# Chunk products of an RWKV-7 recurrence: from tiles of the array to the full array, with both heads moving

## The chip, the cores and the metric

The kernel runs on one core of a Trainium2 chip. The metric is the device time of one execution in microseconds (us). The engines are TensorE (PE in the profile; its weight loads are shown apart as PEld), VectorE (DVE), ScalarE (ACT), GpSimd (POOL) and SyncE (SP), which issues the DMAs. Each takes its own instructions in the order in which they were written.

## The reference

Two layers over 528 tokens (16 learned tokens and 512 of the input) of width 1024. Layer 0 is an RWKV-7 mixer with 32 heads of 64, layer 1 is latent attention with 16 heads. What the change touches is the recurrence of layer 0; for every head it is

```
def step(S, inp):
    r_t, w_t, k_t, v_t, a_t, b_t = inp
    sa = einsum('bhij,bhj->bhi', S, a_t)
    S = S * w_t[:, :, None, :] + sa[..., None] * b_t[:, :, None, :] + v_t[..., None] * k_t[:, :, None, :]
    return S, einsum('bhij,bhj->bhi', S, r_t)
```

ahead of it stand the projections of the tokens to v, k, r and a gate g (each 16 tiles of 128 columns), behind it a normalisation, the gate and an output projection.

## The kernel before

**Recurrence in chunks.** The 528 steps are cut into nine chunks, one of 16 steps (chunk 0) and eight of 64. The 32 heads go in 16 pairs; head 0 of a pair lies on partitions 0 to 63 (`H0`), head 1 on 64 to 127 (`H1`). For each pair p the work goes through these stages, each a Python generator that yields small steps:

- `prepare` makes from k, r, the decays and the rates the operands `KB` and `ALR` of all chunks;
- `within` calls `products(p)`: per chunk and head a product of `KB` and `ALR`, masked on DVE into `Qf` (the triangular matrix M to be inverted), `MR` and a part of `ALR`;
- `sides` makes `SV` (state and values) and `KBt`;
- `invert(0)` and `invert(1)` are two lanes that invert M in fp16 by doubling, chunks 0 to 3 and 4 to 8; the last product of a lane writes the inverse over `Qf` (event `within`);
- `ends(0)`, `recur` and `ends(8)` call `chunk` for chunk 0, for chunks 1 to 7 and for chunk 8. A chunk has the products `ALR` by `SV` (into `xs`), `SV` by `ALR` (output), `Qf` by `xs` (into `SV`), `KBt` by `SV` (the next state), `SV` by `MR` (output). The first, third and fourth depend on one another. Chunk 8's output addition sets the event `recur`, and `finish` normalises.

Every chunk product is fp32 and is made of two matmuls, one for each head, on a part of the array: 128 rows by 64 columns, or 64 by 64. One such matmul is two records in the trace. The inverses are fp16 on 128 by 128, the projections fp32r on 128 by 128 with 264 moving columns, three matmuls in a row for each piece (`pg<-x,w`).

**Buffers.** `tl(n, shape, tag)` takes the next of n buffers. `Qf` and `MR` have three, so `products(p)` waits for the event `recur` of pair p-3 (`within`).

**Order.** `Flow` records the instructions and picks, step by step, the one with the earliest start by its own table of costs (`cost`, `LAGS`); between equals the stage that stands first in the list wins (finish, recur, ends, sides, invert, within, prepare, ..., projections last). `hungry` brings a wide matmul forward by `AHEAD`. The order is then fixed in the program. The projections of k and r for pair p can't run far ahead, since `out_k` waits for the event `prepare` of pair p-2. The 16 gate projections come after the last r.

Of the kernel before, what the change touches and what calls it, by code (L numbers as in the profile page):

```python
# [60 lines left out]
class K:  # L61
# [14 lines left out]
    def consts(self):  # L76
        nc = self.nc
        cp = self.cp = self.pool("consts", 1)
        self.par = cp.tile([128, Par.n], F32, name="par")
        self.ones, self.ident, self.center = (cp.tile([128, 128], F32, name=n) for n in ("ones", "ident", "center"))  # L80
        self.bones = cp.tile([128, 128], F32R, name="bones")
        self.omka = cp.tile([128, NP], F32, name="omka")
        nc.gpsimd.memset(self.ones, 1.0)
        for name, x in (("eps_gn", GN_EPS), ("one", 1.0), ("eps_rms", RMS_EPS)):
            t = cp.tile([128, 1], F32, name=name)
            setattr(self, name, t)
            nc.gpsimd.memset(t, x)
# [41 lines left out]
class Flow:  # L129
# [9 lines left out]
    SLACK = 0.0  # L139
# [80 lines left out]
    def cost(eng, method, out, ins, point):  # L220
# [3 lines left out]
        if eng == "tensor":  # L224
# [7 lines left out]
            if w.dtype == F32:  # L232
                if m == 64 and out.base_partition():
                    return [(0.02, m / 1.2e3, 2 * n * r)]
                return [(n / 1.2e3, m / 1.2e3, (2 if m > 64 else 1) * n * r)] * 2
# [99 lines left out]
    def run(self, stages):  # L335
        stages = [[g, None, None] for g in stages]
        while True:
            best, known = None, len(self.events)
            for i, s in enumerate(stages):
# [20 lines left out]
                for j in range(len(s[1])):  # L360
# [3 lines left out]
                    if s[1][j].wide and self.hungry(t):  # L364
                        t -= self.AHEAD
# [33 lines left out]
class Layer0:  # L399
# [57 lines left out]
    def norm(self):  # L457
# [3 lines left out]
        for bufs, tag, n in ((2, "SV", 2), (2, "KBt", 2), (3, "MR", 2), (1, "KB", 2), (3, "ALR", 3), (3, "ALR", 3)):  # L461
            t = tl(bufs, (128, 576 * n), tag)
            wide += [t[:, 576 * i : 576 * i + 576] for i in range(n)]
        wide += [tl(2, (128, 529), "vx") for _ in range(2)]
# [11 lines left out]
        part = [tl(1, (128, T), "P"), tl(2, (128, T), "gx")]  # L476
# [33 lines left out]
    def place(self):  # L510
# [3 lines left out]
        for bufs, tag, n in ((2, "SV", 2), (2, "KBt", 2), (3, "MR", 2), (3, "MR", 2), (3, "ALR", 3)):  # L514
            t = tl(bufs, (128, 576 * n), tag, R)
            wide += [t[:, 576 * i : 576 * i + T] for i in range(n)]
        qf = [tl(3, (128, T), "Qf", R) for _ in range(3)]
        self.lora = {4: qf[0], 5: tl(1, (128, T), "bvl", R)}
        self.spare = wide.pop(10)
        self.places = wide + qf[1:] + [tl(2, (128, T), "Y", R) for _ in range(2)]  # L520
# [45 lines left out]
    def units(self):  # L566
# [5 lines left out]
        self.feed.third([u[0] for u in self.feed.units[0][:AHEAD]], lambda: self.tl(1, (128, 512), "yl"))  # L572
# [47 lines left out]
    def out_v(self, j, out):  # L620
        o = self.tl(2, (128, T), "gx")
# [93 lines left out]
    def out_g(self, p, out):  # L715
# [8 lines left out]
        if p >= 8:  # L724
            if p >= 10:
                yield self.flow.until(("gate", p - 2))
            s = tl(2, (128, T), "gx")
# [60 lines left out]
    def prepare(self):  # L788
        g, nc, tl = self.g, self.nc, self.tl
        yield self.flow.until(("lerps", 0), ("lerps", 1), "decays2")  # L790
        for p in range(NP):
# [53 lines left out]
            ALR = s["ALR"] = tl(3, (128, 9, 3, 64), "ALR")  # L845
            nc.gpsimd.memset(KB[:, 0, :, NM:64], 0.0)
            nc.gpsimd.memset(ALR[:, 0, :, NM:64], 0.0)
            yield
            for x, y, s0 in ((tmp, IP, 1), (kk, at, 0)):
# [6 lines left out]
            for hs, z, eng in ((H0, 0, nc.vector), (H1, 2, nc.gpsimd)):  # L856
# [4 lines left out]
            nc.vector.tensor_tensor(ALR[:, 1:9, 1, :], xm, P[:, 1:9, 1:65], ALU.mult)  # L861
            nc.gpsimd.tensor_tensor(ALR[:, 0, 1, 0:NM], x0, P[:, 0, 1 : NM + 1], ALU.mult)
            yield
# [11 lines left out]
    def within(self):  # L875
        for p in range(NP):
# [3 lines left out]
            if p >= 3:  # L880
                yield self.flow.until(("recur", p - 3))
# [53 lines left out]
    def products(self, p):  # L935
# [4 lines left out]
        MR = s["MR"] = tl(3, (128, 9, 2, 64), "MR")  # L940
        M = s["Qf"] = tl(3, (128, 9, 64), "Qf")
        self.flow.cut[M.tensor.name] = CUT * 64
        nc.gpsimd.memset(MR[:, 0, :, NM:64], 0.0)
        nc.gpsimd.memset(M[:, 0, NM:64], 0.0)
        flat = lambda t: t.rearrange("p s t -> p (s t)")
        for c0 in (1, 5):
# [3 lines left out]
            for j in range(4):  # L950
                for i, hs in enumerate((H0, H1)):
                    nc.tensor.matmul(qv[i][:, j, :, :], flat(KB[hs, c0 + j]), ALR[hs, c0 + j, i : i + 2, :], start=True, stop=True)
# [8 lines left out]
        for i, hs in enumerate((H0, H1)):  # L961
            q = self.one()
            gm.append((q, q[:, 0 : 2 * NM].rearrange("p (s t) -> p s t", t=NM)))
            nc.tensor.matmul(gm[i][1], flat(KB[hs, 0]), ALR[hs, 0, i : i + 2, 0:NM], start=True, stop=True)
        yield
        for i, (q, v) in enumerate(gm):
            for dst, src, m in self.masked(i, M[:, :, 0:NM], MR[:, :, :, 0:NM], ALR[:, :, :, 0:NM], 0, v.unsqueeze(1)):
# [3 lines left out]

    def masked(self, i, M, MR, ALR, cs, qv):

        hs, other, z = ((H0, H1, 0), (H1, H0, 2))[i]
        return ((M[hs, cs, :], qv[hs, :, i, :], self.mS[hs]), (MR[:, cs, i, :], qv[:, :, 1 - i, :], self.mI),
                (ALR[other, cs, z, :], qv[other, :, i, :], self.mS[other]))
# [46 lines left out]
    def inverse(self, p, lane):  # L1023
# [6 lines left out]
        nc.scalar.activation(Mh, M, AF.Copy)  # L1030
        yield
        for hs in (H0, H1):
            nc.gpsimd.tensor_tensor(Lb[hs, :, hs], M[hs], Mh[hs], ALU.subtract)
# [65 lines left out]
        nc.vector.scalar_tensor_tensor(M, v, -1.0, Q, ALU.mult, ALU.subtract)  # L1099
# [4 lines left out]
    def chunk(self, p, ci, small, xs, y, taken):  # L1104
# [3 lines left out]
        ALR, SV, KBt, MR, Qf = (s[x] for x in ("ALR", "SV", "KBt", "MR", "Qf"))  # L1108
        PC = s["PC"][:, ci : ci + 1]
        n = NM if ci == 0 else 64  # L1110
        heads = ((H0, 0), (H1, 1))
        q = small()
        x = q[:, 0:64]
        nc.tensor.matmul(x[H0], ALR[:, ci, 0, :], SV[:, ci, 0, :], start=True, stop=True)
        nc.tensor.matmul(x[H1], ALR[:, ci, 2, :], SV[:, ci, 1, :], start=True, stop=True)
        nc.vector.tensor_copy(xs, x)
        if ci < 8:
            nc.last(x)
        if ci:
            v = y() if ci < 8 else q[:, 64:128]  # L1120
            for hs, h in heads:
                nc.tensor.matmul(v[hs], SV[hs, ci, h, :], ALR[hs, ci, 1, 0:n], start=True, stop=(ci == 8))
            if ci == 8:
                nc.scalar.activation(s["Y"][:, T - 64 :], v, AF.Copy)
# [7 lines left out]
        for hs in (H0, H1):  # L1132
            nc.tensor.matmul(x[hs], Qf[hs, ci, :], xs[hs], start=True, stop=True)
# [4 lines left out]
        if ci < 8:  # L1138
            x = small()[:, 0:64]
            nc.tensor.matmul(x[H0], KBt[:, ci, 0:64], SV[:, ci, 0, :], start=True, stop=True)  # L1140
            nc.tensor.matmul(x[H1], KBt[:, ci, 64:128], SV[:, ci, 1, :], start=True, stop=True)
            for hs, h in heads:
                if ci:
                    nc.vector.scalar_tensor_tensor(SV[hs, ci + 1, h, :], x[hs], PC[hs], sd[hs], ALU.mult, ALU.add)
                else:
                    nc.vector.tensor_scalar(SV[hs, ci + 1, h, :], x[hs], PC[hs], None, ALU.mult)
# [3 lines left out]
        for hs, h in heads:  # L1150
            nc.tensor.matmul(v[hs], SV[:, ci, h, :], MR[:, ci, h, 0:n], start=(ci in (0, 8)), stop=True)
# [4 lines left out]
    def recur(self):  # L1156

        nc, tl = self.nc, self.tl
        for p in range(NP):
# [3 lines left out]
            for cs in ((1, 2, 3, 4), (5, 6, 7)):  # L1163
                yp = self.psum("py", 512, 1)
                for i, ci in enumerate(cs):
# [3 lines left out]
                    def taken(y):  # L1169
                        if ci == cs[-1]:  # L1170
                            n = 64 * len(cs)
                            t0 = NM + 64 * (cs[0] - 1)
                            nc.scalar.activation(Y[:, t0 : t0 + n], yp[:, 0:n], AF.Copy)
                            nc.last(yp)

                    yield from self.chunk(p, ci, small, tl(2, (128, 64), "xs"), lambda: yp[:, 64 * i : 64 * i + 64], taken)

    def ends(self, ci):

        nc, tl, flow = self.nc, self.tl, self.flow  # L1180
        for p in range(NP):
# [9 lines left out]
            def taken(y):  # L1191
                if ci == 0:
                    nc.scalar.activation(Y[:, 0:NM], y, AF.Copy)
                else:
                    nc.vector.tensor_tensor(Y[:, T - 64 :], Y[:, T - 64 :], y, ALU.add)
# [3 lines left out]
            yield from self.chunk(p, ci, self.one, tl(2, (128, 64), "xs"), lambda: self.one()[:, 0 : 64 if ci else NM], taken)  # L1199

    def finish(self):
        g, nc, tl = self.g, self.nc, self.tl
        for p in range(NP):
# [7 lines left out]
            for q, v, ts in (yield from self.headsum(sq, "bvl", "yl", nc.gpsimd)):  # L1211
# [952 lines left out]
```

## Time and profile before

| | us |
|---|---|
| median of three runs | 1615.7 (1611.27 to 1623.01) |
| the profiled execution, its own time | 1630.59 |
| its span, first to last instruction | 1628.6 |
| PE busy in the span | 1498.6 (92%) |
| DVE, ACT, POOL busy | 1006.9, 967.1, 806.3 |

Up to about 206 us the kernel projects v and prepares, from there to 993 us it runs the recurrence with the projections of k, r and g between, and after that the output projection and layer 1. Busy time of PE is modelled from pipelined records, so the distance from one start to the next tells more than a record's own duration. All instructions carry the line of the recording helper (L293), so that groups are told apart by the names of their tiles, as out<-moving,stationary.

### The profile page before, as it was taken

The numbers are of one execution on the slowest core, as the hardware profiler recorded it, in microseconds if no ns is written. First come the engines' busy times: TensorE is split into PE (matmuls) and PEld (weight loads), VectorE is DVE, ScalarE is ACT, GpSimd is POOL, SyncE is SP. The second block draws the span as 40 slices with busy tenths as digits, with TensorE's granted clock in tenths as the row PEclk, the third lists the DMA queues.
The fourth block names the chain that finished last, engine by engine and source line by source line (L and its number), as shares of the span: only waits on it lengthen the run. The fifth ranks groups of instructions, "written<-read, shape, count | busy, mean of one in ns | idle before, by whom it ended". The sixth has DMA issues, their size and how long they took to land. (4 is left out here: it accounts for less than half of the span.)

```text
span 1628.6 us, 36087 instructions
## 1 busy us (share of the span) xinstructions
PE 1498.6 (92%) x13788; PEld 1292.3 (79%) x13788; DVE 1006.9 (62%) x2144; ACT 967.1 (59%) x2451; POOL 806.3 (50%) x1039
## 2 busy tenths in 40 slices
PE   4889889999999999998899999999989999999997
PEld 3889878777877877777787889998778888877786
DVE  7994677788778678777664542035366666666503
ACT  3557657876767677775686865445454544544532
POOL 5353566566556465554565565745522222332554
PEclk8999999999989899998897999999989999999999
DMA  3446522122112121121402247532211111111332
GB/s 112 143 173 230 188 85 87 41 68 74 68 58 71 42 77 65 61 81 55 167 35 73 86 139 256 159 110 92 68 52 40 56 46 52 59 56 43 110 93 82
DMA packets 84700, 148.66 MB, mean 91 GB/s; under 512 B 9392, under 2 KB 18480, under 8 KB 84528
## 3 DMA queue, kind: packets, MB, share of 16 engines
q1 hardware_dynamic: 84528, 146.37, 27.7%
q8 instruction: 108, 1.77, 0.4%
q14 instruction: 64, 0.52, 0.1%
HBM read 112.87 MB, written 33.46 MB: 90 GB/s over the span
## 5 line engine op out<-in xcount | busy, mean ns | idle before, releaser
L293 POOL TENSOR_TENSOR w<-wraw,w 128x512 fp32r<-128x512 f32 (+1 forms) x278 | 358.7, 1296 | 431.3 <-ACT w L293 393.5
L293 PE MATMUL pg<-x,w 128*128 128x264 f32 x2256 | 401.7, 310 | 5.3 <-ACT k L293 3.9
L293 PEld LDWEIGHTS pg<-x,w 128*128 128x128 f32 x2256 | 313.1, 196 | 21.1 <-ACT k L293 4.9
L293 ACT ACTIVATE w<-wraw 128x512 fp32r<-128x512 f32 (+1 forms) x278 | 169.6, 616 | 154.1 <-DMA wraw<-wo 51.0
L293 POOL TENSOR_TENSOR sd<-SV,PC 64x64 f32<-64x64 f32 x224 | 80.7, 360 | 73.8 <-DVE SV L293 63.9
L293 PE MATMUL pb<-u,w 128*128 128x512 f32 x384 | 106.4, 410 | 5.3 <-DVE sg L293 5.3
L293 PE MATMUL pg<-lat,w 128*128 128x512 f32 (+1 forms) x480 | 109.4, 370 | 0.0
L293 DVE SCALAR_TENSOR_TENSOR SV<-pc,PC,sd 64x64 f32<-64x64 f32 x224 | 63.2, 282 | 55.3 <-PE pc L293 49.0
L293 PEld LDWEIGHTS pg<-lat,w 128*128 128x128 f32 x480 | 82.2, 201 | 10.6
L293 PEld LDWEIGHTS pb<-u,w 128*128 128x128 f32 x384 | 71.4, 196 | 19.6 <-DVE sg L293 6.0
L293 PE MATMUL pg<-O,w 128*128 128x512 f32 x336 | 81.7, 401 | 1.8 <-DVE O L293 1.2
L293 ACT ACTIVATE SV<-pc 64x64 f32<-64x64 f32 x224 | 48.4, 216 | 49.5 <-PE pc L293 41.0
L293 PEld LDWEIGHTS pg<-O,w 128*128 128x128 f32 x336 | 63.8, 192 | 17.1 <-DVE O L293 2.0
L293 PEld LDWEIGHTS <-Mb 128*128 128x128 f16 x1152 | 51.9, 98 | 20.8 <-issue 4.5
L293 DVE TENSOR_TENSOR Xs<-pw,masks 128x128 f16<-128x128 f32 (+1 forms) x160 | 48.0, 305 | 30.5 <-PE pw L293 18.6
L293 POOL TENSOR_TENSOR Lb<-Qf,Mh 64x256 f16<-64x256 f32 (+1 forms) x64 | 50.7, 793 | 28.4 <-ACT Mh L293 23.9
L293 DVE SCALAR_TENSOR_TENSOR sg<-sg,par,rs 128x264 f32<-128x264 f32 x32 | 15.6, 518 | 73.5 <-ACT rs L293 73.5
L293 ACT ACTIVATE Qb<-pw 128x256 f16<-128x256 f32 (+1 forms) x128 | 51.8, 410 | 15.3 <-PE pw L293 13.7
L293 PE MATMUL pw<-Tm,Mb 128*128 128x32 f16 (+1 forms) x864 | 55.8, 183 | 4.9 <-DVE Tm L293 4.2
L293 ACT ACTIVATE PT<-py 128x128 fp32r<-128x128 f32 (+1 forms) x64 | 27.9, 436 | 53.6 <-PE py L293 53.6
L293 ACT ACTIVATE Tm<-pw 128x128 f16<-128x128 f32 (+1 forms) x160 | 44.9, 288 | 24.2 <-PE pw L293 22.0
L293 DVE TENSOR_TENSOR sg<-sg,rs 128x256 f32<-128x256 f32 x12 | 7.1, 596 | 72.8 <-ACT rs L293 72.8
(396 smaller groups left out, 3857.6 us busy)
## 6 DMA issues: line engine op xcount, KB each, us to landing
wraw<-wr SPq DMA_DIRECT2D x120, 256.0 KB, 2.7
wraw<-wo SPq DMA_DIRECT2D x64, 256.0 KB, 2.7
wraw<-wi SPq DMA_DIRECT2D x46, 256.0 KB, 2.6
d_v<-gx SPq DMA_DIRECT2D x16, 264.0 KB, 2.1
d_c<-o SPq DMA_DIRECT2D x16, 264.0 KB, 2.2
d_a<-vx SPq DMA_DIRECT2D x16, 264.0 KB, 2.8
c<-d_c SPq DMA_DIRECT2D x16, 264.0 KB, 2.9
a<-d_a SPq DMA_DIRECT2D x16, 264.0 KB, 3.3
```

The lines of the kernel that those rows point to most:

```text
L293: getattr(eng, method)(*args, **kw)
```

## The change

Each chunk product becomes one matmul on the full array: the stationary operand holds both heads, the moving operand too, and of the 128 by 128 result only the two diagonal blocks of 64 are read. `Qf` becomes block diagonal (128 wide, with zeros in the other blocks), `ALR` gets a fourth part so that the parts for both heads lie side by side. What read one tile of 128 partitions now reads two blocks with an instruction each: `xs` (head 1 goes to ACT), the outputs `Y`, the cast `Mh`, the last step of an inverse. `Qf` and `MR` have two buffers instead of three, and `within` waits for `recur` of pair p-2. Other tags change too (`gx` has one buffer, the gate's `s` of pairs 8 and up takes `vx` and waits for the last pair's `sides` and `prepare`, `yl` is gone). In `Flow`, a wide matmul is put back by `DEFER` as long as the recurrence isn't finished, `SLACK` is 0.05, and the activity count of fp32 matmuls is one for all.

```diff
-    SLACK = 0.0
+    SLACK, DEFER = 0.05, 0.12
...
-                    if s[1][j].wide and self.hungry(t):
-                        t -= self.AHEAD
+                    if s[1][j].wide:
+                        t += -self.AHEAD if self.hungry(t) else 0.0 if "finished" in self.events else self.DEFER
...
     def out_v(self, j, out):
-        o = self.tl(2, (128, T), "gx")
+        o = self.tl(1, (128, T), "gx")
...
+            for hs, z in ((H0, 3), (H1, 2)):
+                nc.gpsimd.memset(ALR[hs, :, z, :], 0.0)
+                yield
...
-            nc.vector.tensor_tensor(ALR[:, 1:9, 1, :], xm, P[:, 1:9, 1:65], ALU.mult)
+            for hs, z in ((H0, 2), (H1, 3)):
+                nc.vector.tensor_tensor(ALR[hs, 1:9, z, :], xm[hs], P[hs, 1:9, 1:65], ALU.mult)
...
-            if p >= 3:
-                yield self.flow.until(("recur", p - 3))
+            if p >= 2:
+                yield self.flow.until(("recur", p - 2))
             yield from self.products(p)
...
-        MR = s["MR"] = tl(3, (128, 9, 2, 64), "MR")
-        M = s["Qf"] = tl(3, (128, 9, 64), "Qf")
+        MR = s["MR"] = tl(2, (128, 9, 2, 64), "MR")
+        M = s["Qf"] = tl(2, (128, 9, 128), "Qf")
+        for hs, other in ((H0, H1), (H1, H0)):
+            nc.gpsimd.memset(M[hs, :, other], 0.0)
...
-        nc.scalar.activation(Mh, M, AF.Copy)
+        for hs in (H0, H1):
+            nc.scalar.activation(Mh[hs], M[hs, :, hs], AF.Copy)
...
-        nc.vector.scalar_tensor_tensor(M, v, -1.0, Q, ALU.mult, ALU.subtract)
+        for hs in (H0, H1):
+            nc.vector.scalar_tensor_tensor(M[hs, :, hs], v[hs], -1.0, Q[hs], ALU.mult, ALU.subtract)
...
-        x = q[:, 0:64]
-        nc.tensor.matmul(x[H0], ALR[:, ci, 0, :], SV[:, ci, 0, :], start=True, stop=True)
-        nc.tensor.matmul(x[H1], ALR[:, ci, 2, :], SV[:, ci, 1, :], start=True, stop=True)
-        nc.vector.tensor_copy(xs, x)
+        x = q[:, 0:128]
+        nc.tensor.matmul(x, flat(ALR[:, ci, 0:2]), flat(SV[:, ci]), start=True, stop=True)
+        nc.vector.tensor_copy(xs[H0], own(x, 0))
+        nc.scalar.activation(xs[H1], own(x, 1), AF.Copy)
...
-        for hs in (H0, H1):
-            nc.tensor.matmul(x[hs], Qf[hs, ci, :], xs[hs], start=True, stop=True)
+        nc.tensor.matmul(x, s["Qf"][:, ci, :], xs, start=True, stop=True)
...
-            nc.tensor.matmul(x[H0], KBt[:, ci, 0:64], SV[:, ci, 0, :], start=True, stop=True)
-            nc.tensor.matmul(x[H1], KBt[:, ci, 64:128], SV[:, ci, 1, :], start=True, stop=True)
+            nc.tensor.matmul(x, KBt[:, ci, :], flat(SV[:, ci]), start=True, stop=True)
...
-        for hs, h in heads:
-            nc.tensor.matmul(v[hs], SV[:, ci, h, :], MR[:, ci, h, 0:n], start=(ci in (0, 8)), stop=True)
+        nc.tensor.matmul(v, flat(SV[:, ci]), MR[:, ci, :, 0:n], start=(ci in (0, 8)), stop=True)
...
+                            for h, hs in enumerate((H0, H1)):
+                                nc.scalar.activation(Y[hs, t0 : t0 + n].rearrange("p (c t) -> p c t", t=64), yv[hs, :, h, :], AF.Copy)
```

In PE's queue, this is a chunk of pair 8 before: the output of one chunk (`py<-MR,SV`), the first two products of the next, a piece of a projection, and the product with `Qf`. A trailing "64x64 x2" is two matmuls, one a head.

```order
L293 MATMUL pw_1968_9835<-ident_60,KB_1838_9111 128x128 x4
L293 MATMUL py_1956_9778<-MR_1720_8479,SV_1803_8926 64x64 x2
L293 MATMUL pc_1971_9864<-SV_1803_8926,ALR_1693_8289 64x64 x2
L293 MATMUL py_1956_9778<-ALR_1693_8289,SV_1803_8926 64x64 x2
L293 MATMUL pg_1932_9645<-x_374_1243,w_1914_9527 128x264
L293 MATMUL pg_1932_9645<-x_375_1244,w_1914_9527 128x264
L293 MATMUL pg_1932_9645<-x_374_1243,w_1915_9528 128x264
L293 MATMUL pc_1975_9878<-xs_1970_9863,Qf_1721_8480 64x64 x2
```

And this is the same place of a chunk (of pair 5) in PE's queue now.

```order
L294 MATMUL py_1587_7652<-MR_1341_6273,SV_1338_6270 128x128
L294 MATMUL pc_1624_7817<-SV_1338_6270,ALR_1264_5826 128x128
L294 MATMUL py_1587_7652<-ALR_1264_5826,SV_1338_6270 128x128
L294 MATMUL pw_1613_7769<-inv_1609_7745,bones_62 128x264
L294 MATMUL pw_1614_7770<-inv_1609_7745,bones_62 128x264
L294 MATMUL pw_1613_7769<-P_1610_7746,bones_62 128x264
L294 MATMUL pw_1614_7770<-P_1610_7746,bones_62 128x264
L294 MATMUL pc_1628_7833<-xs_1623_7816,Qf_1342_6274 128x64
```

Each pair of matmuls on a part of the array has become one on all of it, so that between its neighbours the shape doesn't change; over the whole queue the array's shape changes 159 times, before 1213 times.

The second place is the start of `products` of pair 8 in PE's queue before (`pw<-ALR,KB`). `SV_1528_7369` and `KBt_1529_7370` belong to pair 6, whose chunk 4 still runs there; its chunk 8 (`pw_1800_8896<-MR_1458_7017`) stands 268 rows later.

```order
L293 MATMUL pw_1726_8490<-Xs_2393,Qb_1396 128x32
L293 MATMUL pw_1722_8481<-ALR_1693_8289,KB_1692_8288 128x128
L293 MATMUL pw_1723_8482<-ALR_1693_8289,KB_1692_8288 128x128
...
L293 MATMUL pc_1727_8506<-SV_1528_7369,KBt_1529_7370 64x64 x2
L293 LDWEIGHTS o_645_2360
L293 MATMUL pw_1728_8508<-Qb_1396,o_645_2360 128x64
```

Now they stand behind the last chunk of pair 6 (`MR_1485_7037`, `SV_1482_7034`) and the first full chunk of pair 7.

```order
L294 MATMUL pw_1754_8544<-MR_1485_7037,SV_1482_7034 128x128
L294 MATMUL pw_1762_8580<-SV_1654_7979,ALR_1523_7275 128x128
L294 MATMUL pg_1746_8508<-x_367_1234,w_1678_8114 128x264
L294 MATMUL pg_1746_8508<-x_368_1235,w_1678_8114 128x264
...
L294 MATMUL pg_1747_8509<-x_367_1234,w_1679_8115 128x264
L294 MATMUL pw_1769_8590<-ALR_1692_8160,KB_1691_8159 128x128
L294 MATMUL pw_1770_8591<-ALR_1692_8160,KB_1691_8159 128x128
```

From the first row of these products to the last chunk of the same pair there are 1365 rows of PE's queue before and 998 now. In all, ACT has 2629 instructions (2389 before), DVE 2210 (2146), POOL 1140 (1044) and SP 589 (589).

## Rows read from the trace of the kernel before

**Rows 1.** Busy time by stretch; columns PE, PEld, DVE, ACT, POOL, granted clock, DMA.

```profile
364.70:709.60 344.90, 327.21 (x4244) 269.05 (x4241) 266.31 (x681) 250.98 (x732) 200.75 (x352) 0.96 0.20 64
...
709.60:957.00 247.40, 234.27 (x2685) 194.27 (x2682) 151.68 (x381) 172.24 (x471) 134.32 (x204) 0.90 0.26 87
...
993.40:1628.60 635.20, 589.53 (x3510) 514.31 (x3509) 296.75 (x598) 290.35 (x639) 255.73 (x216) 0.97 0.26 81
206.30:993.40 787.10, 746.11 (x9101) 622.88 (x9098) 552.95 (x1373) 561.83 (x1573) 456.16 (x739) 0.95 0.24 79
```

**Rows 2.** Timeline of PE from 440 us: start, duration, group, records.

```profile
439.94 0.61 PE L293 MATMUL pg<-x,w 128*128 128x264 f32 x3
440.39 0.60 PE L293 MATMUL pw<-ident,KB 128*128 128x128 f32 x4
440.92 0.34 PE L293 MATMUL py<-MR,SV 128*64 128x64 f32 x4
441.19 0.29 PE L293 MATMUL pw<-Qb,o 128*128 128x64 f16 x4
```

**Rows 3.** Timeline of PE from 613 us, in a chunk of pair 8.

```profile
615.91 0.34 PE L293 MATMUL py<-MR,SV 128*64 128x64 f32 x4
616.08 0.29 PE L293 MATMUL pc<-SV,ALR 128*64 128x64 f32 x4
...
616.55 0.63 PE L293 MATMUL pg<-x,w 128*128 128x264 f32 x3
617.12 0.33 PE L293 MATMUL pc<-xs,Qf 64*64 64x64 f32 x4
...
617.49 0.61 PE L293 MATMUL pg<-x,w 128*128 128x264 f32 x3
617.94 0.29 PE L293 MATMUL pw<-Xs,Qb 128*128 128x32 f16 x5
```

**Rows 4.** Timeline of PE in layer 1: fp32 on the full array between projections.

```profile
1076.27 0.53 PE L293 MATMUL pd<-y,w 128*128 128x264 f32 x3
1076.63 0.60 PE L293 MATMUL pc<-acc,ones 128*128 128x264 f32 x2
1077.07 1.05 PE L293 MATMUL pc<-sqh,ones 128*128 128x264 f32 x4
```

**Rows 5.** Groups by shape on ACT, 364.7 to 709.6 us: busy, mean ns.

```profile
L293 ACT ACTIVATE SV<-pc 64x64 f32<-64x64 f32 x110 | 23.7, 216 | 19.0 <-PE pc L293 12.9 <-POOL sd L293 2.0 <-PE pw L293 1.3
...
L293 ACT ACTIVATE Mh<-Qf 128x320 f16<-128x320 f32 x8 | 3.7, 466 | 0.1
...
L293 ACT ACTIVATE Mh<-Qf 128x256 f16<-128x256 f32 x8 | 3.3, 414 | 1.4 <-DVE Qf L293 1.3
...
L293 ACT ACTIVATE Y<-py 128x256 f32<-128x256 f32 x8 | 3.1, 382 | 3.4 <-PE py L293 3.3
```

**Rows 6.** The same for DVE.

```profile
L293 DVE TENSOR_TENSOR ALR<-r,P 128x512 f32<-128x512 f32 x8 | 6.2, 777 | 0.1
...
L293 DVE SCALAR_TENSOR_TENSOR Qf<-pw,Q 128x320 f32<-128x320 f32 x8 | 3.9, 488 | 1.5 <-ACT SV L293 0.8 <-PE pw L293 0.6
```

**Rows 7.** Groups by shape on POOL, whole span.

```profile
L293 POOL MEMSET ALR<- 128x144 f32 x16 | 3.6, 223 | 0.0
...
L293 POOL MEMSET Pfirst<- 96x512 f32 x1 | 0.5, 532 | 0.0
```

**Rows 8.** Timelines: products of pair 8 begin; chunk 8 of pairs 6 and 8 ends.

```profile
537.98 1.87 PE L293 MATMUL pw<-ALR,KB 64*128 64x128 f32 x14
...
564.63 0.22 DVE L293 TENSOR_TENSOR Y<-Y,pw 128x64 f32<-128x64 f32 x1
...
652.09 0.21 DVE L293 TENSOR_TENSOR Y<-Y,pw 128x64 f32<-128x64 f32 x1
```

**Rows 9.** Issues of DMAs on the page: KB each, us to landing.

```profile
d_v<-gx SPq DMA_DIRECT2D x16, 264.0 KB, 2.1
```

More of the change, by code (lines that the diff above doesn't have):

```diff
@@ L460, in norm @@
         wide = []
[L461 removed]
+        for bufs, tag, n in ((2, "SV", 2), (2, "KBt", 2), (2, "MR", 2), (1, "KB", 2), (3, "ALR", 4), (3, "ALR", 4)):
             t = tl(bufs, (128, 576 * n), tag)
             wide += [t[:, 576 * i : 576 * i + 576] for i in range(n)]
[L464 removed]
         xs, self.u = [], []
@@ L513, in place @@
         wide = []
-        for bufs, tag, n in ((2, "SV", 2), (2, "KBt", 2), (3, "MR", 2), (3, "MR", 2), (3, "ALR", 3)):
+        for bufs, tag, n in ((2, "SV", 2), (2, "KBt", 2), (2, "MR", 2), (3, "ALR", 4), (2, "Qf", 2), (2, "Qf", 2)):
             t = tl(bufs, (128, 576 * n), tag, R)
             wide += [t[:, 576 * i : 576 * i + T] for i in range(n)]
[L517 to L520, printed above, removed]
+        self.lora = {4: wide.pop(10), 5: wide.pop(10)}
+        self.places = wide + [tl(1, (128, T), "bvl", R), tl(2, (128, T), "Y", R)]
+        self.spare = tl(2, (128, T), "Y", R)
     def lerps(self, lane):
@@ L970, in products, with masked @@
         yield
[L972 to L976, printed above, removed]
+    def masked(self, i, M, MR, ALR, cs, qv, n=64):
+        hs, other = ((H0, H1), (H1, H0))[i]
+        return ((M[hs, cs, hs.start : hs.start + n], qv[hs, :, 0, :], self.mS[hs]), (MR[:, cs, i, 0:n], qv[:, :, 1, :], self.mI),
+                (ALR[other, cs, i, 0:n], qv[other, :, 0, :], self.mS[other]))
     def side(self, p):
@@ L1107, in chunk @@
         s = self.st[p]
-        ALR, SV, KBt, MR, Qf = (s[x] for x in ("ALR", "SV", "KBt", "MR", "Qf"))
+        ALR, SV, KBt, MR = (s[x] for x in ("ALR", "SV", "KBt", "MR"))
         PC = s["PC"][:, ci : ci + 1]
@@ L1191, in taken @@
             def taken(y):
[L1192 to L1195, printed above, removed]
+                n = 64 if ci else NM
+                for h, hs in enumerate((H0, H1)):
+                    v = y[hs, h * n : h * n + n]
+                    if ci == 0:
+                        nc.scalar.activation(Y[hs, 0:NM], v, AF.Copy)
+                    else:
+                        nc.vector.tensor_tensor(Y[hs, T - 64 :], Y[hs, T - 64 :], v, ALU.add)
+                if ci:
                     nc.event(("recur", p))
                 nc.last(y)
-            yield from self.chunk(p, ci, self.one, tl(2, (128, 64), "xs"), lambda: self.one()[:, 0 : 64 if ci else NM], taken)
+            yield from self.chunk(p, ci, self.one, tl(2, (128, 64), "xs"), lambda: self.one()[:, 0 : 128 if ci else 2 * NM], taken)
     def finish(self):
@@ L1210, in finish @@
             rs = None
-            for q, v, ts in (yield from self.headsum(sq, "bvl", "yl", nc.gpsimd)):
+            for q, v, ts in (yield from self.headsum(sq, "bvl", "gx", nc.gpsimd)):
                 if rs is None:
```

59 lines of the change are left out of this document (31 added, 28 removed).

## The prediction

> **What bounds the kernel now.** I read the stretches first. From the first product of `KB` and `ALR` to the last gate projection (206.3 to 993.4 us) PE is busy for 746.1 of 787.1 us; in eight pairs from the middle (pairs 4 to 11, 344.9 us) for 327.2, against 266.3 on DVE, 251.0 on ACT and 200.8 on POOL [rows 1]. That is 43.1 us a pair, of which PE 40.9, DVE 33.3, ACT 31.4, POOL 25.1. PE is the limit, and only 17.7 us in eight pairs are left without it. So I then read the timeline of PE for what its time goes into, from the start of one group to the start of the next.
>
> Three matmuls of a projection take 0.45 us when a group on the full array follows (617.49 to 617.94, 439.94 to 440.39) and 0.57 when a chunk product on part of the array follows (616.55 to 617.12) [rows 2, 3]. Four transposes on the full array take 0.53 with a chunk product behind them (440.39 to 440.92) where 0.60 - 0.27 = 0.33 us lie between the starts of the first and the last, so 0.11 for each and 0.44 for four: 0.09 is left over [rows 2]. The chunk product itself takes 0.27 until a group on the full array starts (440.92 to 441.19), but 0.17 until another of the same shape does (615.91 to 616.08) [rows 2, 3]: 0.10 left over. So each change of the array's shape costs PE about 0.095 us, in and out, and it doesn't matter here what kind of number follows: from a projection to fp32 on the full array there is none (439.94 to 440.39).
>
> The Trainium skill says the same, in TensorEngine Tiling (Array Packing), section Tiling Modes: a change of mode drains the array.
>
> **The change part by part.** *Shapes.* The queue of PE changes shape 1213 times before and 159 times now, by count of the order. 1054 x 0.095 = -100 us, all of it on the engine that bounds this part.
>
> *The product.* In place of 0.17 for a pair of matmuls there is one with 128 columns. Its two records aren't in this trace. The nearest row is fp32 with 264 columns: two records from 1076.63 to 1077.07, 0.22 each [rows 4], so 0.83 ns a column and 0.107 for 128; the transposes with 128 columns take 0.11 [rows 2]. I take 0.22 a product; there are 43 for each pair (seven chunks with five, two with four), 688 in all: 688 x 0.05 = +34 us. The product with `Qf` has only 64 columns (a fifth of them, 144): it may cost 0.11 instead of 0.22, if its weights come in time, which would be 144 x 0.11 = 16 us less. I don't count on that.
>
> *Weight loads beside it.* A projection that follows a change of shape starts with weights that weren't loaded ahead. 206 chunk products have a projection behind them before, and no change of shape there now; in turn 164 full loads now stand behind short fp16 matmuls, which hide little. Each is at most 0.1 us (a load of 128 columns lasts no longer than the 0.11 of such a record): -21 to +16 us, I take -5. PE's work: -100 + 34 - 5 = -71 us, or 4.4 a pair.
>
> *More instructions on the others.* ACT gets 240 more: 144 copies of `xs` at 0.216, 32 casts `Mh` at 0.414 or 0.466 (half the partitions, the same columns for each), 32 outputs `Y<-py` at up to 0.382, 32 small ones at up to 0.216 [rows 5]: 31 + 14 + 12 + 7 = 64 us, 4.0 a pair. DVE gets 64 more: 16 `ALR<-r` at 0.777, 32 last steps of the inverse at up to 0.488 [rows 6], 16 additions `Y<-Y,pw` at 0.21 [rows 8]: 12 + 15 + 3 = 30 us, 1.9 a pair. POOL gets 64 memsets of 576 columns; 144 columns take 0.223 and 512 take 0.532 [rows 7], so 0.58 for 576: 37 us, with 32 small instructions some 44, 2.8 a pair. A pair then holds 40.9 - 4.4 = 36.5 us on PE, 35.4 on ACT, 35.2 on DVE, 27.9 on POOL. PE is still first, but the others have come level, and a copy of `xs` on ACT now waits behind whatever ACT does. So PE will wait more often than for 5% of the time. If the share of waits stayed, a pair would take 38.4 us; if it rose to what leaves nothing of the gain, 43.1. I take 8%: 36.5 / 0.92 = 39.7, or 3.4 less than now. 16 pairs: -55 us. This is the term on which the forecast rests.
>
> *Two places.* Products of pair 8 begin at 538.0, while chunk 8 of pair 6 ends at 564.9 [rows 8]; the new wait forbids that. From the start of the products to the end of chunk 8 a pair now takes 652.3 - 538.0 = 114 us. With two places a pair of pairs can't be faster than one passage. In PE's queue the passage of pair 8 shrinks from 1365 rows to 998, because the inverse of pair 8 no longer stands behind that of pair 7. PE works off rows 2935 to 7049 of its queue in the 344.9 us of [rows 1], 0.084 us a row, so 998 rows are 84 us, and 75 with 2 x 4.4 off for PE's cheaper work. Two pairs in 79.4 us, as forecast, leave 4 us for waits beyond today's. I count nothing more here; what it costs if the passage stays long is the first rival.
>
> *Deferred projections* cost nothing as long as PE has other work: about seven gate projections are left behind the last chunk instead of five, work that PE must do anyway. *One `gx`*: its DMA lands 2.1 us after issue [rows 9], while v projections of 48 matmuls (16 x 0.45 us = 7 us) lie between evacuations; without that cover, 16 x 2.1 = 34 us. *The gate's `s` in `vx`* waits for the last pair, but the gates concerned are the last eight, which mostly stand behind it in the order anyway. *SP* has as many DMAs as before. Layer 1 is untouched: 635 us [rows 1].
>
> *The clock.* It was at 0.95 in this part and 0.90 from 709.6 to 957 us [rows 1]. PE gets the same projections in less time, so I expect it no lower; bounds -20 to +15 us, I take 0.
>
> **Sum.** The profiled execution took 1630.6 us: 1630.6 - 55 = 1575.6. The median of the runs shown is 14.9 below that execution, so 1560.7; I take 1560.
>
> **The rivals.** *Slower: the passage of a pair stays long.* If a pair still needs 95 us or more from its products to its end, two places allow a pair each 47.5. The first two pairs aren't bound so; 14 x (47.5 - 43.1) = +62, 1692 on the scale of the profile, 1677 as a median. It decides from 86 us on (2 x 43.1). For it: the 114 us of today, and a chain of products each of which now waits for a weight load of 128 columns and for ACT too. Against it: the 998 rows, and that today's passage is stretched by a PE that is busy 95%. Chance 0.14.
>
> *No gain: ACT and DVE take PE's place.* They are busy 73% and 77% in the middle [rows 1]. If a chain this tight can't use ACT above 82%, a pair takes 35.4 / 0.82 = 43.2 and all is lost in waits on PE: 1630.6, or 1616. Chance 0.11.
>
> *More gain.* PE waits no more than now, `Qf` products cost half, the clock keeps up: -71 - 16 - 10 and up to 10 off the waits, some -97 to -105: 1513 to 1519 as a median. Chance 0.2.
>
> *The tiles were the better form.* Were the 0.095 due to something that stays, only the +34, the -5 and the 16 of waits (71 - 55) would be left: +45, 1660 as a median. Were a product on the full array twice the 0.17, 0.34, it would be 688 x 0.17 = +117 with -100, -5 and +16: +28, 1644. The 0.45 from a projection to fp32 on the full array speaks against the first, the 0.107 worked out of [rows 4] against the second. Chance 0.03 for both.
>
> The Trainium skill (same page, Performance Considerations) holds column tiling to be the form for 64 stationary columns, up to twice as fast; that is the second of these two cases. The pair at 0.17 against about 0.22 agrees in sign, not in size.
>
> **How the numbers follow.** The forecast has 0.52: from 1535 (PE waits stay at 5%) to 1590 (waits of 13%). With the greater gain 0.2, no gain 0.11, slower 0.17. The range that leaves out 2 in 10 goes from 1508, below the greater gain, to 1635, above no gain and a few of the slower cases. One per cent, 16 us, is what a measurement of this kernel tells from no change: faster by more 0.74, within 0.11, slower by more 0.15.
>
> **What would show it.** Right: chunk products on PE are two records 0.11 apart, projections of three take 0.45 beside them, the pairs follow each other in about 40 us, and ACT and DVE are busy near 90% in the middle. Wrong in the first step: gaps of 0.1 us around full-array products. Wrong in the third: PE idle for 15% or more in the middle, waiting for `xs`, `SV` or steps of the inverse, with the products of a pair starting right behind `Y<-Y,pw` of the last but one and pairs 43 us or more apart. The place of the forecast that is most likely to fail is the 8%.

## The result, and the profile after

The changed kernel takes 1693.1 us (median of 4 runs, 1687.6 to 1693.3), the kernel before 1616.7: a ratio of 1.0463, interval 1.0419 to 1.0507. The forecast was 1560, the range 1508 to 1635: wrong in size and in direction. The profiled execution has a span of 1691.5 us, 62.9 more than the profiled execution of before, which lay 14 us above its own median. Ratios, here and below, are taken from runs in the fast state alone; of all runs only one, of before_count_only (1691.2 us), was a slow one.

I read the same stretches as in [rows 1], and the one from the first product to the last gate projection, which now ends at 1057.8 us instead of 993.6. Busy time by stretch, columns as there:

```profile
364.70:709.60 344.90, 297.74 (x3142) 261.93 (x3142) 239.20 (x621) 253.08 (x750) 187.57 (x348) 0.95 0.18 57
...
206.30:1057.80 851.50, 743.62 (x7701) 659.93 (x7700) 572.99 (x1436) 632.14 (x1811) 489.53 (x833) 0.95 0.23 73
```

The last line tells most of it. PE works 743.6 us where it worked 746.1 [rows 1], at the same granted clock of 0.95: the 71 us of saved work aren't there. And it stands idle for 851.5 - 743.6 = 107.9 us where it stood for 41.0 [rows 1]. What is left behind the stretch, layer 1 above all, takes 1691.5 - 1057.8 = 634 us, where it took 635 [rows 1]. Neither ACT nor DVE fills the hole: in the 344.9 us of the first line (seven pairs now, eight before) both are busy for less than 254.

What sets the pace is seen where a pair starts. The last step of chunk 8 of pair 6, on DVE, and the products of pair 8, on PE (timelines; [rows 8] shows the same places of before):

```profile
584.77 0.45 DVE L294 TENSOR_TENSOR Y<-Y,pw 64x64 f32<-64x64 f32 x2
...
586.19 1.26 PE L294 MATMUL pw<-ALR,KB 64*128 64x128 f32 x12
```

Before, these products began 27 us ahead of that step [rows 8]; now 1 us behind it, and in all of pairs 4 to 11 between 0.4 and 3.0 us behind it. A passage (from the products to the end of chunk 8) takes 97 us on the mean of these pairs, two pairs are under way, and a pair follows each 49.5 us instead of 43.5 (from the products of pair 4 to those of pair 14).

Some of the longest waits in the same 344.9 us (us in total, times, longest; the first line is that of before) point to a chain in which each engine waits for another, and not to one engine that is short of time:

```profile
POOL sd L293 <- DVE SV L293: 24.3, 20, 3.7
...
POOL sd L294 <- DVE SV L294: 57.8, 29, 7.8
ACT xs L294 <- DVE xs L294: 21.0, 17, 4.2
...
PEld pc L294 <- ACT xs L294: 12.4, 29, 0.9
...
PEld pc L294 <- ACT SV L294: 10.5, 26, 1.5
```

Why PE's work didn't fall is seen in a chunk of pair 8 (timeline of PE, answering to [rows 3]):

```profile
654.86 0.47 PE L294 MATMUL pc<-SV,KBt 128*128 128x128 f32 x2
655.09 0.61 PE L294 MATMUL pg<-x,w 128*128 128x264 f32 x3
655.54 0.38 PE L294 MATMUL py<-MR,SV 128*128 128x128 f32 x2
...
657.36 0.61 PE L294 MATMUL pg<-x,w 128*128 128x264 f32 x3
657.81 0.38 PE L294 MATMUL pc<-SV,ALR 128*128 128x128 f32 x2
658.06 0.49 PE L294 MATMUL py<-ALR,SV 128*128 128x128 f32 x2
...
660.62 0.43 PE L294 MATMUL pc<-xs,Qf 128*128 128x64 f32 x2 [0.24 <-ACT xs L294]
660.89 0.25 PE L294 MATMUL pw<-Xs,Qb 128*128 128x32 f16 x4
```

From start to start, three projections take 0.45 ahead of a chunk product, as forecast, and a product 0.23 (654.86). But `Qf` with 64 columns takes 0.27, and the product after 657.81 begins only 0.25 later. The weight loads (groups on PEld in 364.7 to 709.6 us: busy, mean ns, idle before; the first line is that of before):

```profile
L293 PEld LDWEIGHTS pg<-x,w 128*128 128x128 f32 x768 | 108.1, 195 | 6.5 <-ACT k L293 1.0 <-ACT r L293 0.3
...
L294 PEld LDWEIGHTS pc<-SV,ALR 128*128 128x128 f32 x102 | 16.3, 199 | 5.6 <-issue 3.2 <-PE py L294 1.8
...
L294 PEld LDWEIGHTS pc<-xs,Qf 128*128 128x128 f32 x102 | 15.8, 195 | 13.8 <-ACT xs L294 12.4
L294 PEld LDWEIGHTS pc<-SV,KBt 128*128 128x128 f32 x100 | 15.5, 195 | 11.7 <-ACT SV L294 10.5
```

A load of 128 columns is on record with 0.195 to 0.2 us, not the 0.11 that I took as its bound, and a product has two of them. The trace of before had the same 0.195 for a projection's load. That record isn't what a load costs, though: three projections with such loads take 0.45, so a part of it overlaps with other work. What it costs can be read from the products themselves. The load of the `Qf` product at 660.62 starts with the product, as `xs` comes, and not ahead of it. In the products of `KBt` the first of the two records lasts 0.21 us until the second starts (median), in those of `SV` by `ALR` that go into `py` 0.11. That the difference is a load which nothing hides is likely, not shown. Over all records of the stretch (from the start of one to the start of the next, cut off at its own end, which adds up to the busy time above) a product takes 0.287 us (197.4 / 688) where its tiles took 0.263 (181.1 / 688, drains behind it included). By kind, the medians are 0.22 (`ALR` and `SV` into `py`), 0.25 (`SV` and `ALR`), 0.27 (`Qf`), 0.30 (`MR`) and 0.33 (`KBt`): the forecast's 0.22 holds for one kind of the five.

### The profile page after: what moved, and what is told of

The parts are those of the page before. It is cut to its first block, busy times and chain, and to the rows that moved or that the text cites. A ratio compares the mean times of both kernels' runs of the same rounds, so it can differ in the third digit from the quotient of the medians.

```text
span 1691.5 us, 33974 instructions
## 1 busy us (share of the span) xinstructions
PE 1497.0 (89%) x12412; PEld 1329.5 (79%) x12412; DVE 1034.2 (61%) x2208; ACT 1041.4 (62%) x2691; POOL 844.8 (50%) x1135
## 5 line engine op out<-in xcount | busy, mean ns | idle before, releaser
L294 PE MATMUL pg<-x,w 128*128 128x264 f32 x2112 | 376.2, 309 | 7.6 <-POOL w L294 3.2
L294 PEld LDWEIGHTS pg<-x,w 128*128 128x128 f32 x2112 | 296.2, 197 | 11.3 <-POOL w L294 3.4
L294 ACT ACTIVATE w<-wraw 128x512 fp32r<-128x512 f32 (+1 forms) x278 | 169.9, 616 | 131.6 <-DMA wraw<-wo 62.9
L294 POOL TENSOR_TENSOR sd<-SV,PC 64x64 f32<-64x64 f32 x224 | 76.2, 340 | 129.1 <-DVE SV L294 119.5
L294 PEld LDWEIGHTS <-Mb 128*128 128x128 f16 x1152 | 62.0, 101 | 40.6 <-issue 17.8
L294 PE MATMUL pc<-SV,KBt 128*128 128x128 f32 x224 | 56.0, 333 | 14.5 <-ACT SV L294 12.7
L294 DVE TENSOR_TENSOR Xs<-pw,masks 128x128 f16<-128x128 f32 (+1 forms) x160 | 47.5, 304 | 33.6 <-PE pw L294 15.8
L294 PE MATMUL pc<-xs,Qf 128*128 128x64 f32 x224 | 49.1, 302 | 19.1 <-ACT xs L294 17.8
L294 PEld LDWEIGHTS pc<-xs,Qf 128*128 128x128 f32 x224 | 35.5, 198 | 31.4 <-ACT xs L294 29.4
L294 PE MATMUL pc<-SV,ALR 128*128 128x128 f32 x224 | 49.9, 306 | 9.1 <-DVE SV L294 8.6
```

Source lines behind the costliest of these rows:

```text
L294: getattr(eng, method)(*args, **kw)
```

## The experiments

All times are medians, each with its ratio to the kernel before run beside it.

**Two places alone.** The kernel before with the new wait in `within`:

```
-            if p >= 3:
-                yield self.flow.until(("recur", p - 3))
+            if p >= 2:
+                yield self.flow.until(("recur", p - 2))
```

> The kernel before with one line changed: products of pair p wait for the end of pair p-2 (two places in use), all products and buffers as before. Theory P (two places cost the time): after the change a pair takes 94 to 102 us from its products to its end and two pairs share that; with the old products, PE has more to do, so 100 to 110 us, a pair every 50 to 55, 14 pairs x 6 to 11 us more than 43.7: 1700 to 1770 us. Theory Q (the full-array products and the copies on ACT lengthen the chain, the places do no harm): 1605 to 1630, as before.

1683.0 us, 1.0401 (1.0362 to 1.0440): theory P's direction, below its 1700. Pair 6 ends and pair 8 starts:

```profile
594.80 0.21 DVE L293 TENSOR_TENSOR Y<-Y,pw 128x64 f32<-128x64 f32 x1
...
597.52 1.16 PE L293 MATMUL pw<-ALR,KB 64*128 64x128 f32 x16
```

The wait alone, with the old products, costs nearly what the whole change costs, but not in the same way: 28 us of it is idle time of PE and 26 us a lower clock (last section).

**The wait moved forward.** The changed kernel; the places are written over, and the first products wait for chunk 4 only:

```
-            if p >= 2:
-                yield self.flow.until(("recur", p - 2))
+            if p >= 2:
+                yield self.flow.until(("chunk", p - 2, 4))
...
+            if c0 == 5 and p >= 2:
+                yield self.flow.until(("recur", p - 2))
```

> The changed kernel with one edit: the two places of MR and Qf stay, but the products of chunks 1 to 4 of a pair wait only for chunk 4 of the pair before the last, and those of chunks 5 to 8 and 0 for its end as before. (So that this is free of a handover of whole tiles, the two places are allocated once and written over; the zero quarters of Qf are then set in the first two pairs only, which takes 28 memsets of 576 columns from POOL.) Theory P, two places cost because products of a pair can't begin before chunk 8 of the pair before the last: products begin four chunks of about 5.2 us, 21 us, earlier, two pairs take 98 - 21 = 77 us instead of 98 where nothing else binds, so PE's own work binds again: 39.7 to 43 us a pair, 1570 to 1620 us. Theory A, ACT and DVE have come level with PE and bind at 43 us a pair: 1616 to 1645 us. Theory R, the loss lies in the products themselves: 1660 us or more.

1650.7 us, 1.0211 (1.0179 to 1.0242): 42 us of the 76 come back, by this wait and the memsets that went with it. That is P's direction, not its size, and neither A nor R. The wait and the memsets weren't tried apart. The products now begin 9 us ahead of the end of the pair before the last (mean of pairs 4 to 11), not the 21 that P had, and a passage still takes 99 us. A pair now follows each 44.9 us and the recurrence ends at 963.4 us, where it ended before. The rest stands behind it: 387 matmuls of gate projections (50.5 us) instead of 240 (30.5). The stretch to the last of them:

```profile
206.30:1014.50 808.20, 723.59 (x7700) 643.52 (x7698) 575.17 (x1436) 630.41 (x1809) 473.00 (x790) 0.97 0.24 77
```

PE is idle for 84.6 us on the way and has those projections left at the end. Of the 43 us that this stretch is shorter than in the changed kernel, 23 are idle time; the other 20 are work on the same products and projections, at a granted clock of 0.97 instead of 0.95.

**Does the deferral cost that?** `SLACK, DEFER` at 0, first in the changed kernel, then in the one with the early wait, and 0.05 with half the deferral.

> The changed kernel with SLACK and DEFER at 0, as the planner was before. Theory P: the passage of a pair is set by the two places, the order of projections matters little: 1680 to 1705. Theory R (the projections held back leave PE empty): 1650 or less.

1718.1 us, 1.0620 (1.0579 to 1.0661), slower by 25 us than the changed kernel, and above P's range.

> The kernel after_early_products (1650.7 us) with SLACK and DEFER at 0. There the recurrence ends at the same 963 us as in the kernel before, but some 50 us of projections are left behind it instead of 30, while PE has stood idle for 84 us on the way. Theory D (deferral now costs what it leaves behind): the idle time is filled, 1610 to 1640 us. Theory C (projections ahead of the chain lengthen it, as with two places and the late wait, where no deferral was 25 us slower): 1660 to 1690 us.

1697.8 us, 1.0510 (1.0486 to 1.0534).

> The kernel after_early_products with DEFER 0.05 instead of 0.12. Theory D: between it and early_no_defer, 1625 to 1645 us. Theory C: 1650 to 1670 us. If it is slower or faster than both neighbours by more than 10 us, the order of the planner scatters by that much for any small change of its numbers.

1683.3 us, 1.0422 (1.0394 to 1.0451). So 1698, 1683, 1651 for a DEFER of 0, 0.05, 0.12 with the early wait: theory D falls, and the first two are above theory C's ranges too. The passages of pairs 6 to 11 grow to between 115 and 124 us without deferral. That a projection ahead of a step of the chain lengthens it (theory C) isn't shown as the reason: the granted clock falls as the deferral is taken away, and a large part of the loss is work at the lower clock (last section).

**xs on DVE**, in the changed kernel and with the early wait:

```
-        nc.scalar.activation(xs[H1], own(x, 1), AF.Copy)
+        nc.vector.tensor_copy(xs[H1], own(x, 1))
```

> The changed kernel, but both blocks of xs are copied on DVE. Theory P: the copy of head 1 is taken out of ACT's queue (ACT waits for DVE's half 21 us in eight pairs), the second copy takes 0.22 us more on DVE in each chunk; the passage changes by a few us at most: 1675 to 1700. Theory Q (waiting for ACT in each chunk makes the chain long): 0.5 us x 9 chunks a pair, 1650 or less.

1683.4 us, 1.0409 (1.0376 to 1.0441): 10 us.

> The kernel after_early_products with both copies of xs on DVE, in place of one on DVE and one on ACT. In the changed kernel this was worth 10 us while the passage of a pair bound it. Theory P: with the passage off the bound the gain shrinks to 0 to 8 us against after_early_products. Theory A (ACT binds): 10 to 20 us less than after_early_products.

1660.8 us, 1.0272 (1.0238 to 1.0307): 10 us the other way, which neither theory had. The copy's engine isn't the cause of the 76 us.

**Which products.** With the early wait, the three products of the chain (`ALR`, `Qf`, `KBt`) go back into two tiles, and `y` keeps its two on the full array:

```
-        nc.tensor.matmul(x, flat(ALR[:, ci, 0:2]), flat(SV[:, ci]), start=True, stop=True)
+        for hs, h in heads:
+            nc.tensor.matmul(x[hs], ALR[:, ci, h, :], SV[:, ci, h, :], start=True, stop=True)
```

> The kernel after_early_products with the three products that the chain waits for (ALR by SV, Qf by xs, KBt by SV) back in two tiles, and xs copied by DVE in one instruction; the two that end in the output y (SV by ALR, SV by MR) stay on the full array. 416 products change back. Theory L (a full-array product whose weights can't be loaded before its wait costs 0.29 us and not the 0.22 of its two records, against 0.26 for two tiles with the change of shape): PE's work falls by about 10 us, each chunk of the chain by 0.3 us and ACT by 31 us: 1620 to 1645 us. Theory M (the changes of shape are what costs, 0.095 in and out): 416 x (0.19 - 0.05) = 58 us more work, 1680 us or more.

1648.5 us, 1.0227 (1.0172 to 1.0281): no change.

```profile
206.30:1010.80 804.50, 740.68 (x8529) 626.03 (x8527) 564.08 (x1435) 598.48 (x1666) 474.56 (x789) 0.97 0.24 77
```

PE works 17 us more than with all five (740.7 for 723.6), at the same clock, and is idle for 21 us less (63.8 for 84.6). Theory M's 58 us aren't there, nor L's gain. A chain product on the full array saves PE 17 / 416 = 0.04 us, drains of its neighbours included, and the idle time takes it back.

> The kernel early_y_products_full with SLACK and DEFER at 0. Theories L and D together: 1595 to 1625 us, level with the kernel before or faster. C: 1650 us or more.

1698.0 us, 1.0510 (1.0486 to 1.0533): as above, no deferral is worse, and L and D together fall.

**Three places, two full products.** The kernel before, with the products of `ALR` and `KBt` on the full array; then the planner's edits too; then these alone. The first of them also has the new count of fp32 columns in the planner's costs, which its expectation doesn't say.

```
-            nc.tensor.matmul(x[H0], KBt[:, ci, 0:64], SV[:, ci, 0, :], start=True, stop=True)
-            nc.tensor.matmul(x[H1], KBt[:, ci, 64:128], SV[:, ci, 1, :], start=True, stop=True)
+            nc.tensor.matmul(x, KBt[:, ci, :], flat(SV[:, ci]), start=True, stop=True)
```

> The kernel before, but the products ALR by SV and KBt by SV are one matmul on the full array; the xs copy of head 1 is on ACT as after the change; three places, the other three products, all buffers, SLACK and no DEFER as before. The array changes shape 910 times instead of 1213. Theory P: PE bounds the kernel before, so 303 x 0.095 = 29 us less and 272 products x 0.05 = 14 us more, some 10 to 25 us faster: 1590 to 1607. Theory Q: the longer products and the ACT copy stand on the chain of a chunk (three steps, about 0.15 us each for two products and a wait on ACT), slower by 10 to 40 us: 1625 to 1655.

1666.7 us, 1.0306 (1.0274 to 1.0339): slower than either theory had it; the count is in this.

> The kernel two_full_products_three_places (1666.7 us) with SLACK 0.05 and DEFER 0.15 as well, so that it differs from before_planner_edits in the two full-array products (ALR by SV, KBt by SV), the layout of ALR, and the copy of xs on ACT alone. If its loss came from the planner putting projections ahead of the chain: 1570 to 1610 us. If it came from the longer products and from ACT in the chain (theory Q): 1640 us or more, and 20 us or more above before_planner_edits.

1676.9 us, 1.0352 (1.0309 to 1.0396): 19 us above the next run, close to what theory Q asked for.

> The kernel before with the planner's three edits alone: fp32 products of the full array counted once instead of twice, SLACK 0.05 and a DEFER (0.15; 0.12 in the changed kernel). No product, place or buffer is changed. In the changed kernel SLACK and DEFER were worth 25 us, where PE waited for the chain. Here PE is taken 95% and projections are never short of a place: 1600 to 1630 us expected by theory P (no change). If projections ahead of the chain cost here too: 1580 to 1600 us.

1657.5 us, 1.0249 (1.0202 to 1.0297). Not a product or a place is changed in the last, and it is 37 us slower than the kernel before. The planner's numbers, which I had counted at nothing, were a suspect of their own.

**The planner's numbers one by one.** The count in the kernel before, as shown here, the deferral in it, and the old count in the changed kernel. The last two also have a line by which an fp32 product never counts as a projection:

```
-                return [(n / 1.2e3, m / 1.2e3, (2 if m > 64 else 1) * n * r)] * 2
+                return [(n / 1.2e3, m / 1.2e3, n * r)] * 2
```

> The kernel before with one edit of the planner: the columns of an fp32 product with more than 64 stationary columns are counted once instead of twice (SLACK and DEFER 0). Theory S (each number of the planner was set for the order that it gave, and a small change of one gives another order that is some 10 to 40 us worse): 1630 to 1660 us. Theory T (the count doesn't matter, the deferral costs the 37 us of before_planner_edits): 1610 to 1625 us.

1682.4 us, 1.0364 (1.0308 to 1.0420), its runs far apart (1665.6 to 1691.2).

> The kernel before with SLACK 0.05 and DEFER 0.12, as in the changed kernel, and the old count. Theory T: 1645 to 1665 us, with some 60 us of projections left behind the recurrence, which itself ends no later than 963 us. Theory S: anything from 1620 to 1660 us, and not the sum of the two edits' costs.

1666.5 us, 1.0311 (1.0258 to 1.0363).

> The changed kernel with the old count of fp32 columns (a product of 128 columns still doesn't count as a projection). Two places and the late wait stay, so theory P (the passage of a pair binds) expects 1680 to 1705 us, no change beyond the scatter of the order. If the count made the order worse here: 1650 to 1675 us.

1667.7 us, 1.0302 (1.0283 to 1.0322): 25 us less than the changed kernel. On the kernel before the two edits cost about 60 and 49 us alone and 37 together (there with a DEFER of 0.15): they don't add up, as theory S says. How the count makes an order worse wasn't taken apart. Lower clocks go with it: over the whole execution the runs of before_count_only were granted 0.92 to 0.94, the runs of the kernel before beside them 0.96 to 0.97.

**What is left when the suspects are taken out.** First with two places: the kernel of the `y` products with the old count and SLACK 0, and the inverse of the first chunks starts without waiting for the products of chunks 5 to 8.

```
-            yield flow.until(("products", p))
+            yield flow.until(("products", p, lane))
```

> The kernel early_y_products_full with three more edits: the inverse of chunks 0 to 3 starts as soon as the products of chunks 1 to 4 and 0 are there (those of 5 to 8 come last), the old count of fp32 columns, SLACK 0 and DEFER 0.12. If two products on the full array are worth their 272 x 0.14 us of saved changes of shape and the passage no longer binds: 1590 to 1615 us, faster than the kernel before. If they are worth nothing, or two places still cost: 1620 to 1645 us.

1641.3 us, 1.0146 (1.0098 to 1.0193): still 1.5% slower than the kernel before.

Then with three places: two full products with the old count, and `KBt` alone with the old count and a DEFER of 0.12.

> The kernel two_full_products_three_places (1666.7 us) with one edit: the old count of fp32 columns (a product of 128 columns still doesn't count as a projection). If its loss was the count: 1600 to 1635 us. If it is the products (two weight loads of 128 columns each behind a wait, xs on ACT): 1650 us or more.

1655.7 us, 1.0206 (1.0150 to 1.0262): the count was 11 us of this kernel's loss (16 by the ratios), the rest stays.

> The kernel before with one of the five products, KBt by SV, on the full array (and the layout of ALR that goes with the others), three places, the old count, SLACK 0 and DEFER 0.12. 128 products of 688. PE's gain is at most 128 x (0.26 - 0.22) = 5 us, its loss at most 128 x 0.03 = 4 us; so the order decides: 1600 to 1640 us. Below 1605 us it would be a better kernel than the one before.

1610.3 us, 0.9951 (0.9910 to 0.9991): level with the kernel before, by half a per cent the fastest of all. Its stretch:

```profile
206.30:976.50 770.20, 726.66 (x8845) 619.95 (x8842) 539.52 (x1373) 559.19 (x1574) 455.78 (x739) 0.96 0.26 81
```

43.5 us of idle time, 2.5 more than before, and 20 us less work. Some of the 20 is the clock, 0.96 for 0.95, and the profiled execution of before was one of its slower ones; by the medians the gain is 10 us.

## Why the prediction was wrong

**"Two places": the passage estimated at 75 to 84 us.** This step failed first, and the rival "Slower: the passage of a pair stays long" describes what happened (1677 as a median; 1693 measured). I divided PE's queue by PE's pace, as if a passage were as long as PE needs for its rows. But a passage is a chain through PE, DVE, ACT and POOL, and PE waits in it. Where a pair starts as soon as the pair before the last ends, a pair must follow in half a passage; the runs with that wait do so:

| kernel | passage, mean of pairs 4 to 11 | half of it | measured, a pair |
|---|---|---|---|
| changed | 97.4 | 48.7 | 49.5 |
| two_places_old_products | 97.2 | 48.6 | 48.7 |
| after_no_defer | 102.4 | 51.2 | 51.0 |
| after_xs_on_dve | 98.5 | 49.2 | 48.7 |
| after_old_count | 94.6 | 47.3 | 47.5 |
| before (three places) | 108.6 | 54.3 | 43.5 |

The passage did shrink, by 11 us, and 97 is still above the 86 from which I had it decide. The trace of before gave a warning: its shortest passage, of pair 0, takes 95.4 us from 206.6 to 301.9. It was no more than that, for in the changed kernel pair 0 takes 85.2. That the late wait costs time is shown twice, by the edit that makes it alone (1683) and by the one that gives part of it back (1651), and by the places where pairs start. Why a passage takes 97 us and not 75 to 84 wasn't taken apart.

**"The product" and "Weight loads beside it": -71 us of work.** The drains are real: a projection ahead of a product takes 0.123 us where it took 0.213 (medians of the last of a group), and PE's queue has its 1054 changes of shape less. The term that was mis-sized is the product: it measured 0.287 for my 0.22: 688 x 0.067 = +46 us. The rest of the work (projections, inverses, sums) fell by 19 us where -41 was left in my sum. -30 - 41 became +16 - 19, and -71 became -2.6. The bound on a load, "no longer than the 0.11 of such a record", was a wrong reading: 0.195 is on record. And I counted loads only where a projection or a short fp16 matmul stands beside a product, while the products of the chain lose time at their own first record: 0.16 to 0.21 us in the median, where the first records of the products into `py` last 0.11. The Trainium skill (TensorE: Matmul & The Clock Gate, section Weight-path perf modes — Fast Weight Load (FWL) and DoubleRow) says that the faster way of loading weights is for types other than fp32; the trace agrees, with 0.10 for a load of 128 columns of fp16 (`Mb`, mean of 497) and 0.195 for fp32.

**The 8% of waits** became 12.7% (107.9 of 851.5). It goes with the passage. ACT is busy for 74% of that stretch and DVE for 67%, so rival "No gain", in which ACT binds at 82%, doesn't describe it; moving `xs` to DVE gained 10 us in one kernel and lost 10 in another.

**"Deferred projections cost nothing"** failed in sign as well: the deferral helps the changed kernel by 25 us (1718 to 1693), of which 18 are work at a higher clock and 8 idle time, and costs the kernel before some 49. The count of fp32 columns has no place in the prediction at all; it is 25 us of the changed kernel.

**The shares.** Two places with the late wait 42 us, the count 25 us, and the rest open: these are differences of single edits, and the planner's order, and with it the clock, changes with each, so they aren't added up to the 76. An edit that changes no instruction (before_count_only) moved the time by 60 us, so that no single difference of this size is proof of its cause without the trace beside it. The five products by themselves on three places weren't tried, and whether a third place of the wider `Qf` has room isn't shown. With one of them, on three places, the kernel is as fast as before, with two 2% slower, but the planner's SLACK and DEFER differ between these two as well.

**Smaller slips.** By the prediction's own sum, waits of 5% and 13% give 1540 and 1597, not 1535 and 1590, and the greater gain begins at 1511, not 1513. None of this bears on the failure.

**Right:** projections at 0.45, a product of 0.22 to 0.23 in the cases named above, layer 1 and the clock unchanged, and little cost of the one `gx` and the gate's `s` in `vx` (PE waits for ACT's `gx` 5.5 us in all, before 3.3).

## What to carry to other kernels

Before a buffer loses a place, read from the trace how long the work through it holds a place, and divide by the places that stay. Rows of one engine's queue times that engine's pace leave the waits of the chain out (84 us against 97 here). A short passage in the old trace is a warning, not a forecast. Price an instruction that replaces two with its weight loads, and ask for each load whether it can start before what the instruction waits for. Where a greedy planner sets the order, a change of its numbers is an edit like any other: run it alone first. And split every difference into idle time and work, with the granted clock beside the work.

## What the runs showed that I had not expected

One number in the planner's costs, without a changed instruction, makes the kernel before some 60 us slower. A chain product on the full array saves PE 0.04 us and the kernel nothing, while the drain that it avoids is 0.09. And with two places the granted clock in the stretch falls to 0.89 with the old products:

```profile
206.30:1048.50 842.20, 772.68 (x9109) 642.13 (x9107) 542.58 (x1373) 563.87 (x1574) 447.71 (x739) 0.89 0.23 73
```

PE then works 26 us longer on the same instructions (772.7 for 746.1), and that is nearly half of what this kernel loses in the stretch; the other 28 us are idle time. In the changed kernel the clock stayed at 0.95 (such a share is a mean over time: at each moment the trace has 1 or 0.5, which is 2.4 or 1.2 GHz).

The clock explains much of what the deferral does. PE's work and idle time up to the last gate projection:

| kernel | PE works | idle | granted clock |
|---|---|---|---|
| changed | 743.6 | 107.9 | 0.95 |
| after_no_defer | 761.5 | 115.9 | 0.88 |
| after_early_products | 723.6 | 84.6 | 0.97 |
| early_no_defer | 747.8 | 104.8 | 0.93 |
| early_y_products_full | 740.7 | 63.8 | 0.97 |
| early_y_products_full_no_defer | 788.5 | 69.6 | 0.89 |

Without the deferral PE runs through the projections that it has and then has the chain alone. In after_no_defer this is seen once in each pair of the middle. In one of them no projection starts from 521.4 to 541.5 us, and from 524.9 to 545.4 the granted clock is 1.2 GHz (the 25 us before and the 25 us with this gap, columns as in [rows 1]):

```profile
495.00:520.00 25.00, 23.58 (x249) 21.21 (x248) 14.53 (x39) 17.44 (x53) 13.00 (x25) 1.00 0.15 46
520.00:545.00 25.00, 16.96 (x133) 14.87 (x133) 18.71 (x49) 13.92 (x43) 13.57 (x27) 0.60 0.18 59
```

The changed kernel's stretches at 1.2 GHz in the same part last 3 to 7 us, those of after_no_defer 14 to 21. So a deferred projection seems to be of use here as work that keeps PE busy while the chain waits; that it also shortens the chain itself wasn't shown.
